# A hybrid attention and RG-LRU block on one core: the last recurrent block interleaved, silu products moved to the middle, y loaded into freed tiles, and two kinds of transfers given to other queues

## Chip, cores and metric

The kernel runs on one core of one Trainium2 chip. Its time is device microseconds (us) of one execution, median over several runs. The profile is one more execution, recorded by the hardware profiler.

The engines are named as in the profile: PE (TensorE matmuls), PEld (TensorE weight loads), DVE (VectorE), ACT (ScalarE), POOL (GpSimd), SP (SyncE, which here only issues DMA transfers; its instruction stream is SPq).

## What is computed

A sequence of 1024 tokens with 1024 channels goes through one decoder block and a final RMSNorm. Cut to what matters:

```python
h = rmsnorm(x, norm_g) * (1 + scale) + shift
q, k, v, g_attn, xr, g_rnn, m_attn, m_rnn = split(h @ w_in)      # 1024 x 6656
y_attn = sliding_window_attention_with_sinks(rope(q), rope(k), v) * silu(g_attn)
xr = causal_depthwise_conv(xr, conv_w, conv_b)                   # width 4
r = sigmoid(block_diag(xr, wa) + ba);  i = sigmoid(block_diag(xr, wx) + bx)
log_a = -8 * r * softplus(-lam);  a = exp(log_a)
b = sqrt(-expm1(2 * log_a)) * (i * xr)                           # reset at position 0
y_rnn = scan(h[t] = a[t] * h[t-1] + b[t]) * silu(g_rnn)
merged = sigmoid(m_attn) * (y_attn @ w_attn_proj) + sigmoid(m_rnn) * (y_rnn @ w_rnn_proj)
out = rmsnorm(x + gate * (merged @ w_out), final_g)
```

The attention window is 128 tokens in blocks of 128; there are 16 heads and 4 key/value heads. The recurrence has four blocks of 256 channels.

## The kernel before

Every large product is made of float32r parts: a tensor is split into a high part (a cast on ACT, names `wh`, `hh`, `yh`) and the rest (a subtraction on DVE, `wl`, `hl`, `yl`), and three matmuls, high by high, low by high and high by low, stand for one float32 product.

**The input projection** is cut into *pairs*: 23 pairs of 256 output columns, each computed by seven block products (a Strassen form on half sequences and half columns). One product is 12 matmuls at L505 and one *slot* of the planner. For each product DVE forms a sum `ws` (L527), ACT casts it to `wh` (L101) and DVE subtracts to `wl` (L107); the second matmul of the product needs `wl`. The list `pairs` (L1249) sets their order: Q (queries), MA and MR (merge gates, a tanh on ACT only), GR and GA (silu paths: a tanh on ACT and one more DVE operation at L613 for each of four tiles), XR (input of the recurrence).

**The recurrence** runs beside these products. After an XR pair, the convolution (L682 to L697) and the gate matmuls (L778, `pgate`, two sets of 24 per block: one for each half of the block's 256 channels) are followed for each half by `after_gates` (L785): sigmoids into `rz` and `it` (L793, L796), DVE products (L799, L803), tanh (L807), exp and square (L810, L813), DVE (L816), sqrt (L820), DVE (L823), the scan (L828), the product with the silu path `gg` (L832), and the split into `yh` (L835) and `yl` (L839), which are stored to `yh_d` and `yl_d`. Each step that changes ACT's function loads a table first. A planner (`background`, L468) places these steps between the products by its own estimates of load; the order on each engine is then fixed. In the last block (`hb == 3`) the second half's steps are listed behind all of the first half's.

**Attention** starts when the recurrence's steps are all issued (L1317 to L1320). Its tiles lie in the memory that the recurrence gives up. It has 32 steps u of one query block and one key/value head: scores (`s_ps`, L1016), masked maximum (L1024 to L1035), exponentials (L1040), transposition (`pt`, L1054), masks on GpSimd (`phm`, `plm`, L1074), and values (`pv`, L1088). In each step one *filler* product is put between: first the last products of the last pair, from the seventh step on the products of `w_rnn_proj` with `yh` and `yl` (L168, `rp`). For this, `load_y` (L1135) brings y back from DRAM: channel blocks 0 and 1 into halves of the `hha`/`hla` tiles, blocks 2 to 7 into twelve tiles of their own, which exist only once the input projection is done.

**Queues.** All transfers but a few are issued by SP in the program's order, and an SP instruction that waits holds up all behind it. In attention, stores of a product's tiles are put off to the end of a step (`store`, L590).

The tail is the product with `w_attn_proj` beside the merge (L1449 to L1481) and that with `w_out` (L1500), with the last norm.

Of the kernel before, what the change touches and what calls it, by code (L numbers as in the profile page):

```python
# [13 lines left out]
F32R = mybir.dt.float32r  # L14
# [8 lines left out]
P = 128  # L23
S = 1024
D = 1024
KC = 8
# [25 lines left out]
def tile_hybrid_block(ctx, tc, x, pk, rows, posr, posi, invf, c_row, w_ss, w_gate, w_main, w_v,  # L52
# [91 lines left out]
    hh, hl = [], []  # L144
    for kc in range(KC):
        for lst, nm in ((hh, "hh"), (hl, "hl")):
# [512 lines left out]
    def xr_sinks(hb):  # L659
# [15 lines left out]
        def conv(ic):  # L675
            def add(s):
# [25 lines left out]
                waiting[1].extend([[("A", 1.06, 0, base)], slots(1), *[[t_] for t_ in taps]])  # L702
# [44 lines left out]
    def start_gates(hb):  # L747
# [4 lines left out]
        one, two = [], [lambda: ask(hb, 1)]  # L752
        for todo, steps_ in ((one, c0), (two, c1)):
            for i, step in enumerate(steps_):
                todo.extend(step + ([slots(1)] if hb < 3 else []))
                if todo is one and i == 3:
                    todo.append(lambda: gq.append((hb, 1)) or True)
        if hb == 3:
            one.insert(0, lambda: W.setdefault("rush", True))
        waiting[0].extend(one + two)  # L760
# [24 lines left out]
    def after_gates(hb, oc):  # L785
        c, t = 2 * hb + oc, {}

        def tl(n, tag=None, dt=F32):
            t[n] = W["rn"].tile([P, S], dt, tag=tag or n, name=n)
            return t[n][:]  # L790

        def a1():
            A.activation(tl("rz"), W["g", (hb, oc)][0][:], AF.Sigmoid, bias=pcol(PK_BA, c))  # L793

        def a2():
            A.activation(tl("it"), W["g", (hb, oc)][1][:], AF.Sigmoid, bias=pcol(PK_BX, c))  # L796
# [5 lines left out]
        def d2():  # L802
            V.tensor_tensor(out=t["it"][:], in0=t["it"][:], in1=W["xc", hb, oc][2][:],  # L803
                            op=ALU.mult)

# [185 lines left out]
    def load_v(m):  # L991
# [143 lines left out]
    def load_y(c):  # L1135
# [7 lines left out]
        h_ = W["yp"].tile([P, S], F32R, tag="Y", name="yh")  # L1143
        l_ = W["yp"].tile([P, S], F32R, tag="Y", name="yl")
        dma(h_[:], yh_d[c])
        dma(l_[:], yl_d[c])
# [3 lines left out]
    def rp_steps():  # L1150
# [4 lines left out]
        W["yp"] = pool(ctx, "ypool", bufs=12)  # L1155
# [20 lines left out]
        load_y(2)  # L1176
# [72 lines left out]
    pairs = [Q[1], MA[0], Q[2], MA[1], Q[3],  # L1249
# [385 lines left out]
```

## Time and profile before

| | |
|---|---|
| median of 3 runs | 945.71 us (943.57 to 946.53) |
| the profiled execution: its time | 944.47 us |
| the profiled execution: its span | 942.5 us |
| PE busy | 908.1 us, 96% of the span |
| DVE, ACT, POOL busy | 73%, 56%, 10% |
| TensorE clock granted | 0.999 |
| DMA moved | 164.19 MB, mean 174 GB/s |

How to read the rows of a timeline: start in us from the span's start, duration in us, engine, line, operation, output<-input, shapes and count; in brackets how long the engine had been idle before it, and what ended that. A row of the windows view gives, for one stretch, its length and then, for PE, PEld, DVE, ACT and POOL, the busy us and the count of instructions; last come the granted clock, the share of time in which the 16 DMA engines were busy (it can pass 1 by rounding) and the GB/s. In a group row the count follows x, then busy us and the mean ns of one.

### The profile page before, as it was taken

To read this page: it belongs to the slowest core of one execution; us is meant where nothing else is said; L and a number is where in the kernel's file an instruction comes from. 1 tells how busy PE (TensorE), PEld (TensorE's weight loads), DVE (VectorE), ACT (ScalarE), POOL (GpSimd) and SP (SyncE) were. 2 spreads that over 40 slices of the span, in tenths; PEclk is the share of its full clock that TensorE was granted. 3 is DMA by queue.
4 is the path that set the end of the run, shared out by engine and by line. 5 is a ranking of instruction groups with operands and counts; after the bars stand their busy time and mean duration, and the time that the engine had idled before them with its cause. 6 is when DMAs were issued, how large, how long until landed. Compare 5 with 4: busy or idle time off the path is not lost.

```text
span 942.5 us, 12419 instructions
## 1 busy us (share of the span) xinstructions
PE 908.1 (96%) x4261; PEld 750.6 (80%) x4261; DVE 688.8 (73%) x1068; ACT 528.8 (56%) x1036; POOL 89.7 (10%) x129
## 2 busy tenths in 40 slices
PE   5899999999999999999999999989999999999997
PEld 3689777788888788888888778867888888887886
DVE  7977798876668955984688677888999737656522
ACT  7434654455556755866585775877888632212311
POOL 1056000000000000000000000233333300000000
PEclk9999999999999999999999999999999999999999
DMA  8923565753332433352334237897666286436321
GB/s 312 370 68 152 184 223 202 268 189 125 112 112 96 139 136 100 133 212 80 122 112 168 100 134 261 278 342 251 215 198 187 67 304 219 168 118 235 128 79 67
DMA packets 84275, 164.19 MB, mean 174 GB/s; under 512 B 12771, under 2 KB 33251, under 8 KB 84214
## 3 DMA queue, kind: packets, MB, share of 16 engines
q1 hardware_dynamic: 83350, 161.09, 49.8%
q0 software_dynamic: 720, 2.07, 0.6%
q8 instruction: 33, 0.54, 0.2%
q14 instruction: 28, 0.23, 0.1%
q10 hardware_dynamic: 144, 0.26, 0.1%
HBM read 114.00 MB, written 49.78 MB: 174 GB/s over the span
## 4 chain that ended last, share of the span: by engine, by line
PE 75%; ACT 4%; DMA 4%; DVE 4%; issue 2%; SPq 0%; POOL 0%; DVEq 0%; ACTq 0%
PE bk L505 39%; PE rp L168 12%; PE rp L1500 5%; PE pgate L778 5%; PE pmain L1500 4%; PE pmain L168 4%; PE s_ps L1016 3%; PE pv L1088 3%; PE pt L1054 1%; DMA dv<-dv_d 1%; DMA ks<-k_d 1%; DMA r<-w_rp 1%; ACT wh L101 1%; DMA r<-w_main 1%; DVE nl L390 1%
## 5 line engine op out<-in xcount | busy, mean ns | idle before, releaser
L505 PE MATMUL bk<-nh,wl 128*128 128x512 f32 x368 | 143.7, 391 | 2.0 <-DVE wl L107 1.9
L505 PE MATMUL bk<-nh,wh 128*128 128x512 f32 x368 | 143.4, 390 | 0.0
L505 PE MATMUL bk<-nl,wh 128*128 128x512 f32 x368 | 143.2, 389 | 0.0
L107 DVE TENSOR_TENSOR wl<-r,wh 128x512 fp32r<-128x512 f32 x108 | 79.1, 736 | 16.5 <-ACT wh L101 16.5
L101 ACT CAST wh<-r 128x512 fp32r<-128x512 f32 x108 | 66.5, 618 | 33.5 <-DMA r<-w_ap 11.3
L505 PEld LDWEIGHTS bk<-nh,wl 128*128 128x128 f32 x368 | 69.1, 188 | 17.7 <-DVE wl L107 3.1
L505 PEld LDWEIGHTS bk<-nh,wh 128*128 128x128 f32 x368 | 69.1, 188 | 15.2 <-ACT wh L103 0.9
L505 PEld LDWEIGHTS bk<-nl,wh 128*128 128x128 f32 x368 | 69.1, 188 | 14.3
L505 PE MATMUL bk<-hh,wl 128*128 128x512 f32 x184 | 71.7, 390 | 0.4 <-DVE wl L107 0.4
L505 PE MATMUL bk<-hl,wh 128*128 128x512 f32 x184 | 71.6, 389 | 0.0
L505 PE MATMUL bk<-hh,wh 128*128 128x512 f32 x184 | 71.6, 389 | 0.0
L107 DVE TENSOR_TENSOR wl<-ws,wh 128x512 fp32r<-128x512 f32 x80 | 54.1, 683 | 4.0 <-ACT wh L101 4.0
L101 ACT CAST wh<-ws 128x512 fp32r<-128x512 f32 x80 | 48.2, 616 | 4.8 <-DVE ws L527 3.0
L1040 ACT ACTIVATE p<-p,small 128x129 f32<-128x129 f32 x128 | 50.1, 400 | 0.0
L59 POOL DMA_DIRECT2D yh_d<-yh x1 | 0.6, 583 | 482.3 <-ACT yh L835 482.3
L505 PE MATMUL bk<-hha,wl 128*128 128x512 f32 x92 | 36.4, 395 | 5.9 <-DVE wl L107 4.4
L505 PEld LDWEIGHTS bk<-hh,wl 128*128 128x128 f32 x184 | 34.5, 188 | 7.9 <-DVE wl L107 0.8
L505 PEld LDWEIGHTS bk<-hh,wh 128*128 128x128 f32 x184 | 34.5, 188 | 7.2
L505 PEld LDWEIGHTS bk<-hl,wh 128*128 128x128 f32 x184 | 34.5, 188 | 7.1
L1016 PE MATMUL s_ps<-ks,qs 128*128 128x256 f32 (+1 forms) x256 | 37.5, 289 | 0.0
L1517 ACT ACTIVATE o<-xo 128x1024 f32<-128x1024 f32 (+2 forms) x10 | 8.9, 889 | 48.4 <-DVE xo L1516 48.4
L505 PE MATMUL bk<-hla,wh 128*128 128x512 f32 x92 | 35.9, 390 | 0.0
(338 smaller groups left out, 2231.7 us busy)
## 6 DMA issues: line engine op xcount, KB each, us to landing
r<-w_main SPq DMA_DIRECT2D x100, 256.0 KB, 4.0
wada<-w_ss SPq DMA_DIRECT2D x16, 512.0 KB, 8.6
qs<-q_d SPq DMA_DIRECT2D x16, 512.0 KB, 5.4
ks<-k_d SPq DMA_DIRECT2D x24, 192.0 KB, 4.1
xt<-x SPq DMA_DIRECT2D x8, 512.0 KB, 7.2
q_d<-rhi SPq DMA_DIRECT2D x16, 256.0 KB, 3.5
q_d<-rlo SPq DMA_DIRECT2D x16, 256.0 KB, 3.3
wg<-w_gate SPq DMA_DIRECT2D x8, 512.0 KB, 5.0
```

Source lines behind the costliest of these rows:

```text
L101: A.copy(dst[0][:], src)
L107: V.tensor_tensor(out=dst[1][:], in0=src, in1=f32(dst[0][:]), op=ALU.subtract)
L168: mm = T.matmul(ps[hf], ww, xx[kc][hf], start=(kc == 0 and ww is w_h and xx is xh), stop=(kc == KC - 1 and xx is xl))
L390: V.tensor_tensor(out=nl[t][:], in0=xT[t][:], in1=f32(nh[t][:]), op=ALU.subtract)
L505: W["pe"] = T.matmul(ps, ww[:, c], b[kc][xx_], start=(first and kc == 0 and i == 0), stop=(kc == 3 and i == 2), skip_group_check=not first)
L778: W["pe"] = T.matmul(ps[:, SL[hf]], ww[:, c0:c0 + P], xx_[:, SL[hf]], start=(ic == 0 and i == 0), stop=(ic == 1 and i == 2))
L1016: W["pe"] = T.matmul(o, qs[:, j, qc], ks[:, b, k0 + (0 if n else P):k0 + 256], start=(b == 0), stop=(b == 1))
L1040: A.activation(px[:, j, :], px[:, j, :], AF.Exp, bias=sm[:, 0, j:j + 1], accum_out=sm[:, 1, j:j + 1])
L1054: W["pe"] = T.transpose(pt[:, j, :], px[:, j, 0:P], ident[:])
L1088: W["pe"] = T.matmul(pv[:], b, m[:].rearrange("p j q -> p (j q)"), start=(i == 0), stop=(i == len(prods) - 1))
L1500: T.matmul(ps[:, sl], lhs[k][th][:, ts_], w[:, sl], start=(k == 0 and w is h_ and lhs is mh), stop=(k == KC - 1 and lhs is ml))
L1517: A.activation(o[:, sl], xo[:, sl], AF.Square, accum_out=fs[:, i:i + 1])
```

## The change

Six edits, on top of a kernel that computes the same.

1. **The order of the pairs.** The silu pairs GR and GA all stand before the last XR pair or directly ahead of it; MA[2], MA[3] and all MR follow it. One pair (now, as before, MR[3]) is left for attention.
2. **The last recurrent block.** The steps of its two halves are interleaved by a list written by hand, and the second half's `rz`, `it`, `th` and `av` take the buffers of the tags `xa` and `xcl` (convolution results, free after the gate matmuls) and no longer wait for the first half's.
3. **A guard**: a convolution waits in the planner until the buffer that it takes has been used (`W["used", c]`).
4. **y into h tiles.** The tiles `hh4` to `hh7` and `hl4` to `hl7` stay open to the end; y blocks 2 to 5 are loaded into them as soon as the input projection has read them, and block 2 is asked for in slot +6 of the last pair, before the `w_rnn_proj` products. In the tail the merged tensor's blocks 2 to 5 are written there too.
5. **v pieces** (`dv`, `vs`; 128 KB each) are loaded by GpSimd.
6. **Tanh stores in attention** (`smr_d`) are issued by ACT, directly behind the activation that makes the tile.

```diff
-    hb = h_ctx.enter_context(tc.tile_pool(name="hb", bufs=1))
+    hb = ctx.enter_context(tc.tile_pool(name="hb", bufs=1))
...
+                whole[nm, kc] = a[:]
...
-                        store(dst[j][:, SL[th]], t["t"])
+                        dma(dst[j][:, SL[th]], t["t"], A if "att" in W else nc.sync)
...
-                waiting[1].extend([[("A", 1.06, 0, base)], slots(1), *[[t_] for t_ in taps]])
+                waiting[1].extend([lambda: c < 2 or ("used", c - 2) in W,
+                                   [("A", 1.06, 0, base)], slots(1), *[[t_] for t_ in taps]])
...
+            waiting[0].extend(
+                [lambda: W.setdefault("rush", True), *a1, a2, d1,
+                 lambda: gq.append((hb, 1)) or True, a3, d2, a4, a5, lambda: ask(hb, 1), *b1,
+                 d3, b2, e1, b3, e2, b4, b5, a6, e3, d4, b6, d5, e4, d6, a7, e5, d7, e6, b7,
+                 e7])
...
+        beside = {"rz": "xa", "it": "xa", "th": "xcl", "av": "xcl"} if c == KC - 1 else {}
...
-        dma(dv[:], dv_d[g][:, n0:n0 + 2, :])
+        dma(dv[:], dv_d[g][:, n0:n0 + 2, :], G)
...
-        dma(vs[:, lo:, :], vs_d[g][:, n0 - 1 + lo:n0 + 1, :])
+        dma(vs[:, lo:, :], vs_d[g][:, n0 - 1 + lo:n0 + 1, :], G)
...
-        h_ = W["yp"].tile([P, S], F32R, tag="Y", name="yh")
-        l_ = W["yp"].tile([P, S], F32R, tag="Y", name="yl")
+        if c < 6:
+            h_, l_ = whole["hh", c + 2], whole["hl", c + 2]
+        else:
+            h_, l_ = (W["yp"].tile([P, S], F32R, tag="Y", name=n_)[:] for n_ in ("yh", "yl"))
...
-        W["yp"] = pool(ctx, "ypool", bufs=12)
+        W["yp"] = pool(ctx, "ypool", bufs=4)
...
-             XR[0], GR[0], GR[1], XR[1], MA[2], GR[2], MR[0], XR[2], MR[1], MR[2], MA[3],
-             XR[3], GR[3]] + GA + MR[3:]
+    pairs = [Q[1], MA[0], Q[2], MA[1], Q[3], XR[0], GR[0], GA[0], XR[1], GR[1], GA[1], GR[2],
+             XR[2], GA[2], GA[3], GR[3], XR[3], MA[2], MA[3]] + MR
...
-    at_slot(s_last + 2, ("N", 0, 0, lambda: load_r(0)), ("N", 0, 0, lambda: load_y(0)),
-            ("N", 0, 0, lambda: load_r(1)), ("N", 0, 0, lambda: load_y(1)),
-            ("N", 0, 0, lambda: prep_r(0, 0)), ("N", 0, 0, lambda: prep_r(1, 0)))
+    at_slot(s_last + 2, [("N", 0, 0, lambda: load_r(0)), ("N", 0, 0, lambda: load_y(0))],
+            ("N", 0, 0, lambda: load_y(1)), ("N", 0, 0, lambda: load_r(1)), [],
+            [("N", 0, 0, lambda: prep_r(0, 0)), ("N", 0, 0, lambda: load_y(2))],
+            ("N", 0, 0, lambda: prep_r(1, 0)))
...
-        if c < 2:
+        if c < 6:
             mh[c], ml[c] = yh[c], yl[c]
```

On PE the order from the first scores on is the same as before, product by product; between the last gate matmuls and the first scores stand 14 products where there were 12. In the instruction orders below, names carry buffer numbers where they are needed to tell tiles apart.

**First place: the DVE order in the second half's steps of the last recurrent block.** Before, from the second half's first product `rz` on (its operand comes from ACT):

```order
L799 SCALAR_TENSOR_TENSOR rz_4951<-rz_4951,pk_t_75,rbig_77 128x1024
L613 SCALAR_TENSOR_TENSOR c_4944<-c_4944,bk0_68 128x512
L565 TENSOR_TENSOR c_4970<-u2_4922,bk3_71 128x512
L107 TENSOR_TENSOR wl_4947<-r_4824,wh_4946 128x512
L527 TENSOR_TENSOR ws_4976<-ws_4949,r_4824 128x512
L803 TENSOR_TENSOR it_4953<-it_4953,xc_4427 128x1024
```

Now, from the second half's `th` on (`th_4914`, `rz_4888` and `it_4887` belong to the second half, `it_4759`, `th_4782` and `rz_4757` to the first):

```order
L836 SCALAR_TENSOR_TENSOR th_4914<-rz_4888,th_4914 128x1024
L843 SCALAR_TENSOR_TENSOR it_4759<-th_4782,it_4759 128x1024
L566 TENSOR_TENSOR c_4976<-u2_4933,bk3_71 128x512
L107 TENSOR_TENSOR wl_4955<-r_4835,wh_4954 128x512
L528 TENSOR_TENSOR ws_4982<-ws_4957,r_4835 128x512
L566 TENSOR_TENSOR c_5003<-bk1_69,p5_4883 128x512
L107 TENSOR_TENSOR wl_4979<-ws_4957,wh_4978 128x512
L528 TENSOR_TENSOR ws_5006<-r_4837,r_4835 128x512
L848 SCALAR_TENSOR_TENSOR rz_4757<-av_4788,it_4759 128x1024
```

The second half no longer begins behind the first half's last step; steps of both halves alternate, and `wl_4955`, of the sixth product after the last gate matmuls, stands behind two steps that wait for ACT.

**Second place: SP at the start of attention.** Each row is a transfer, with the semaphores for which SP waits ahead of it (DMAHW: transfers issued by SP or ACT, in a rotation of eight; DMASW: those issued by GpSimd, likewise; the others are engines). Before:

```order
L59 DMA sink<-rows 128x16 [waits DMASW5_49,DMAHW5_49,DMASW4_49,PE_49]
L59 DMA ks<-k_d 64x2x256 [waits DMASW7_49,DMAHW6_49,DMASW6_49,PE_49]
L59 DMA ks<-k_d 64x2x256 [waits DMAHW7_49]
L59 DMA qs<-q_d_93 128x4x256 [waits DMASW2_49,DMAHW0_49,DMASW1_49,DMASW0_49]
L59 DMA ks<-k_d 64x2x384 [waits DMAHW1_49]
```

Now:

```order
L59 DMA sink<-rows 128x16 [waits DMASW5_49,DMAHW7_49,DMASW4_49,DVE_49]
L59 DMA ks<-k_d 64x2x256 [waits DMASW7_49,DMASW6_49,DMAHW0_49,DMASW1_49,PE_49]
L59 DMA ks<-k_d 64x2x256 [waits DMAHW2_49]
L59 DMA qs<-q_d_93 128x4x256 [waits DMAHW3_49,DMASW2_49,DMASW0_49]
L59 DMA ks<-k_d 64x2x384 [waits DMAHW4_49]
```

GpSimd issues eight transfers early in the program, and the ninth and tenth are the stores of the last `yh` and `yl`, which raise DMASW0 and DMASW1 a second time. Before, every GpSimd transfer waited for here is one of the eight early ones, and PE is waited for at the last gate matmuls. Now the DVE instruction for which `sink` waits is the last block's `yl` subtraction, and the count of DMASW1 for which the first `ks` waits is the second one, the landing of the `yl` store: with edit 2 the memory that attention takes was last used by that tile.

**Third place: SP and the loads of y.** Before, the loads of y blocks 2 and 3 (`yh_d2`, `yl_d2`, `yh_d3`, `yl_d3`) stand behind the last stores:

```order
L59 DMA smr_d6_115<-c_5540 128x512
L59 DMA dv_5555<-dv_d0_88 128x256
L59 DMA vs_5554<-vs_d0_84 128x256
L59 DMA smr_d7_116<-c_5600 128x512
L59 DMA smr_d7_116<-c_5603 128x512
L59 DMA yh_5626<-yh_d2_119 128x1024
L59 DMA yl_5627<-yl_d2_127 128x1024
L59 DMA yh_5630<-yh_d3_120 128x1024
L59 DMA yl_5631<-yl_d3_128 128x1024
```

Now block 2 follows the key and query loads of steps 6 and 7 (`ks_5380`, `qs_5383`), and block 3 those of steps 8 and 9:

```order
L59 DMA r_5369<-ga_d0_97 128x2x256
L59 DMA ks_5380<-k_d_82 64x2x384 x2
L59 DMA qs_5383<-q_d0_93 128x4x256
L59 DMA hh4_174<-yh_d2_119 128x1024
L59 DMA hl4_175<-yl_d2_127 128x1024
L59 DMA r_5507<-ga_d0_97 128x2x256
L59 DMA ks_5518<-k_d_82 64x2x256 x2
L59 DMA qs_5521<-q_d1_94 128x4x256
L59 DMA hh5_176<-yh_d3_120 128x1024
L59 DMA hl5_177<-yl_d3_128 128x1024
```

Stores and v pieces no longer stand on SP, and the loads of y are earlier against the steps of attention.

More of the change, by code (lines that the diff above doesn't have):

```diff
@@ L140, in tile_hybrid_block @@
     h_ctx = ExitStack()
-    hb = h_ctx.enter_context(tc.tile_pool(name="hb", bufs=1))
+    hb = ctx.enter_context(tc.tile_pool(name="hb", bufs=1))
     b12_ctx = ExitStack()
     b12 = b12_ctx.enter_context(tc.tile_pool(name="b12", bufs=1, side="right"))
-    hh, hl = [], []
+    hh, hl, whole = [], [], {}
     for kc in range(KC):
@@ L804, in d2 @@
                             op=ALU.mult)
+            W["used", c] = True
         def a3():
@@ L1142, in load_y @@
             return
-        h_ = W["yp"].tile([P, S], F32R, tag="Y", name="yh")
-        l_ = W["yp"].tile([P, S], F32R, tag="Y", name="yl")
-        dma(h_[:], yh_d[c])
-        dma(l_[:], yl_d[c])
+        if c < 6:
+            h_, l_ = whole["hh", c + 2], whole["hl", c + 2]
+        else:
+            h_, l_ = (W["yp"].tile([P, S], F32R, tag="Y", name=n_)[:] for n_ in ("yh", "yl"))
+        dma(h_, yh_d[c])
+        dma(l_, yl_d[c])
         yh[c] = [h_[:, SL[0]], h_[:, SL[1]]]
```

33 lines of the change are left out of this document (20 added, 13 removed).

## The prediction

> **What bounds the kernel.** First the page's head, its slices, and the windows view for the stretches that the change touches.
>
> ```profile
> span 942.5 us, 12419 instructions
> PE 908.1 (96%) x4261; PEld 750.6 (80%) x4261; DVE 688.8 (73%) x1068; ACT 528.8 (56%) x1036; POOL 89.7 (10%) x129
> DMA  8923565753332433352334237897666286436321
> ...
> 350.00:400.00 50.00, 50.00 (x222) 41.37 (x221) 37.00 (x48) 35.27 (x48) 0.00 (x0) 1.00 0.33 110
> 524.00:577.00 53.00, 49.70 (x215) 39.45 (x214) 41.65 (x53) 38.07 (x52) 1.31 (x3) 1.00 0.46 162
> 580.00:584.00 4.00, 4.00 (x23) 3.44 (x22) 3.21 (x5) 1.81 (x7) 0.44 (x3) 1.00 0.40 152
> 584.00:604.00 20.00, 20.00 (x114) 17.21 (x112) 18.03 (x35) 16.68 (x57) 3.60 (x7) 1.00 1.00 313
> 604.00:612.00 8.00, 8.00 (x47) 6.97 (x46) 6.51 (x13) 7.27 (x21) 2.69 (x5) 1.00 0.54 180
> 612.00:640.00 28.00, 23.57 (x124) 18.31 (x122) 23.10 (x41) 18.35 (x63) 7.92 (x13) 1.00 1.03 349
> ```
>
> PE is busy 96% of the span, and without a gap in a quiet stretch such as 350 to 400. The change takes no matmul away, so it can only win what PE waits: 942.5 - 908.1 = 34.4 us, most of it at the start and end, which no edit touches. Two places matter: 524 to 577, the last recurrent block (3.3 us idle), and 612 to 640, early attention (4.4 us idle), where the DMA engines are full, while they stood half empty from 604 to 612 and at 0.40 around 582.
>
> A wait costs a little more than its idle time, as the pipelined matmuls start anew. The timeline of PE at the first wait, and then all others from 300 to 577:
>
> ```profile
> 529.51 0.39 PE L505 MATMUL bk<-nh,wh 128*128 128x512 f32 x1
> 530.53 0.50 PE L505 MATMUL bk<-nh,wl 128*128 128x512 f32 x1 [0.63 <-DVE wl L107]
> 530.87 0.40 PE L505 MATMUL bk<-nl,wh 128*128 128x512 f32 x1
> ...
> 550.94 0.50 PE L505 MATMUL bk<-hha,wl 128*128 128x512 f32 x1 [1.08 <-DVE wl L107]
> 560.87 0.50 PE L505 MATMUL bk<-nh,wl 128*128 128x512 f32 x1 [1.23 <-DVE wl L107]
> 567.01 0.50 PE L505 MATMUL bk<-hh,wl 128*128 128x512 f32 x1 [0.35 <-DVE wl L107]
> ...
> 325.58 0.50 PE L505 MATMUL bk<-hha,wl 128*128 128x512 f32 x1 [0.45 <-DVE wl L107]
> ```
>
> Matmuls that do not wait start about 50.00 / 222 = 0.23 us apart. From 529.51 over 530.53 to 530.87 pass 1.36 us in place of 0.45: 0.91 us lost for 0.63 idle, 0.28 more. The last block thus loses 0.63 + 1.08 + 1.23 + 0.35 + 4 x 0.28 = 4.4 us. Each time `wl` was late, and DVE was late because it stood in front of a step that waits for ACT.
>
> **The last block now** (edits 1 and 2). I walk through both engines by the new order. Their spacings, from the second half's steps before the change:
>
> ```profile
> 547.67 1.11 ACT L796 ACTIVATE it<-pgate,pk_t 128x1024 f32<-128x1024 f32 x1
> 559.36 1.28 ACT L820 ACT_TABLE_LOAD   x1
> 560.66 1.06 ACT L820 ACTIVATE th<-th 128x1024 f32<-128x1024 f32 x1
> 561.75 1.23 DVE L823 SCALAR_TENSOR_TENSOR it<-th,it 128x1024 f32<-128x1024 f32 x1 [0.33 <-ACT th L820]
> 562.89 0.68 DVE L107 TENSOR_TENSOR wl<-r,wh 128x512 fp32r<-128x512 f32 x1
> 563.49 2.29 DVE L828 TENSOR_TENSOR_SCAN rz<-av,it 128x1024 f32<-128x1024 f32 x1
> ```
>
> So from start to start: an ACT step of 1024 columns about 1.05, a table load 1.3, a cast 0.5; on DVE 1.14, 0.6 for 512 columns, 2.2 for a scan. Let T be the end of the last gate matmuls. ACT: `rz` and `it` to 2.1; the tanh sink of the product that runs first after T cannot start before 3.0 (a product is 12 x 0.227 = 2.72); cast, `th`, cast; the copy of the second product's result at 5.7; table, exp, square to 9.7; sink, cast, and the next table from 10.65; the first half's sqrt from 11.95 to 13.0. DVE has been waiting in front of `it_4759` since 10.9; that step takes 13.0 to 14.15, a join to 14.8, and `wl_4955` is there at 15.5. Its product, the sixth after T, wants it at 5 x 2.72 + 0.23 = 13.8. **One wait of 1.7 us** remains, 2.0 with the restart. Ahead of T the long steps lie at least one product ahead of their `wl`, and after 15.5 each `wl` comes 0.5 to 1.8 us before its product. Term: 4.4 - 2.0 = **2.4 us won**; bounds 4.4 (no wait) and -1 (as many waits again, which the old order shows to be possible).
>
> From 14.8 to the end stand twelve steps of 0.6, four of 1.14 and two scans: 16.2 us; then `yh` on ACT (1.1) and `yl` on DVE (1.2), which ends at T + 32.2. PE is ready for the first scores after 14 products and the wait: T + 40.0, **7.8 us** later.
>
> **The start of attention** (new wait, from edit 2's buffers). As the second order shows, the first `ks` now waits until the `yl` store has landed. Before, it did not:
>
> ```profile
> 567.38 1.26 SPq L59 DMA_DIRECT2D ks<-k_d  x2
> 569.27 1.22 DVE L839 TENSOR_TENSOR yl<-rz,yh 128x1024 fp32r<-128x1024 f32 x1
> 570.80 0.54 POOL L59 DMA_DIRECT2D yl_d<-yl  x1 [0.68 <-DVE yl L839]
> 577.84 1.00 PE L1016 MATMUL s_ps<-ks,qs 128*128 128x128 f32 x8
> ...
> yl_d<-yl SPq DMA_DIRECT2D x7, 512.0 KB, 2.6
> yl_d<-yl POOLq DMA_DIRECT2D x1, 512.0 KB, 7.2
> ...
> DMA to landing us min/median/max: 4.0/5.4/8.9
> ```
>
> The loads left at 567.38, before `yl` was even computed; the trace thus has 7.35 us from the end of `yl` (570.49) to the scores, of which none was needed. Now the chain is: 0.3 to GpSimd's issue, the store's landing, 0.1, 1.26 for two `ks` issues, the landing of `qs` (the last row is that of `qs`). The store takes 2.6 (same size, issued by SP) to 7.2 (the one that GpSimd issued, while the loads that SP had sent from 567.38 on were under way). I take 3.5, near the first, because SP now has nothing to send meanwhile; for `qs` 4.7, between least and median. Sum 0.3 + 3.5 + 0.1 + 1.26 + 4.7 = 9.9, against 7.8: PE waits **2.1 us**. Bounds: 0.3 + 2.6 + 0.1 + 1.26 + 4.0 - 7.8 = 0.5, and with 7.2 and 8.9, 10.0. Behind the waiting SP stand `w_rp`, y and all later loads; they shift with it.
>
> The Trainium skill, DMA: Bandwidth & Descriptors, section on the anatomy of one DMA on the SWDGE (gpsimd) path, gives 2.0 us plus bytes / 436e3 per transfer, by estimate 3.2 us for 512 KB; the trace's 7.2 disagrees, under load. By the page the wait would be 1.8 us.
>
> **Early attention** (edits 4, 5, 6).
>
> ```profile
> 608.89 1.56 SPq L59 DMA_DIRECT2D smr_d<-c  x2
> 610.50 0.42 SPq L59 DMA_DIRECT2D yh<-yh_d  x1
> ...
> 614.32 1.09 PE L1016 MATMUL s_ps<-ks,qs 128*128 128x128 f32 x8
> 617.85 0.73 PE L168 MATMUL rp<-yh,wh 128*128 128x512 f32 x2 [0.48 <-DMA yh<-yh_d]
> 626.90 0.47 PE L1088 MATMUL pv<-phc,vs 128*128 128x512 f32 x1 [1.44 <-DVE small L1035]
> 639.05 0.47 PE L1088 MATMUL pv<-phc,dv 128*128 128x512 f32 x1 [1.82 <-DMA dv<-dv_d]
> 639.95 1.19 PE L1016 MATMUL s_ps<-ks,qs 128*128 128x256 f32 x8
> 644.99 1.19 PE L1016 MATMUL s_ps<-ks,qs 128*128 128x256 f32 x8
> ...
> 604.25 0.39 POOL L1004 COPY p<-sink 128x4 f32<-128x4 f32 x1 [2.02 <-PE pt L1054]
> ```
>
> A quiet step takes 644.99 - 639.95 = 5.04 us; the four from 614.32 to 639.95 took 25.63, so **5.4 us** were lost. SP stood at the store until 608.89; then y blocks 2 to 7, 6 MB, left from 610.50 on into full DMA engines. The windows show the room missed: (349 - 180) x 8 + (349 - 152) x 4 = 2.1 MB, 6.0 us at 349 GB/s. Now no store blocks SP, and blocks 2 and 3 (2 MB) leave when PE has read `hh4` in the fourth step (some 16 us after the first scores) and behind the next keys (some 24 us), in place of 32.7 us. That takes 2 MB out of the full stretch, enough for all 5.4. Against it, the first keys and queries (1.7 MB) now leave about 5 us nearer to the scores, part of which the gap at 580 swallows. I take 1.4 lost, **4.0 won**; bounds 0 and 5.4. v: GpSimd has 2.02 us free between mask and sink copy, two issues take 0.58 + 0.54; nothing. ACT's stores wait for the transfer eight back, a load issued many us earlier; behind them wait a cast and the next step's copy of `s_ps`; nothing, at most 2 us where y or r lands late.
>
> **The middle.** In 300 to 500 four silu pairs more give DVE 16 steps of 0.6 among its 0.74 load (37.00 of 50). The old first block, with two silu pairs beside it, had one wait of 0.45 (+0.28); three such blocks now: 0.5 lost, bounds -0.7 (none) and 3 (waits as in the last block). The tail's orders are unchanged: 0. Edit 3 costs nothing: it moves steps, no engine waits for it.
>
> **Sum**: 2.4 - 2.1 + 4.0 - 0.5 = 3.8 us won: 944.47 - 3.8 = 940.7 for the profiled execution. That one lies 1.24 below the median of its runs, so 941.9, rounded to **942.0**.
>
> **Rivals.**
> 1. *The DMA engines are the bound, not SP.* All bytes of y, keys and v are still needed by the same step, and 612 to 640 stood at 1.03; then term three is 0: 944.7, on the median's scale 945.9. For it: the later start of the keys. Against it: 2.1 MB of unused room. The skill's DMA: Bandwidth & Descriptors, section "Issuing engines are not separate DMA queues", speaks for it: several issuers share 16 engines and save only issue time; the shares of 1.00 and 1.03 agree.
> 2. *The wait at the first scores decides* and makes it **slower**: store 7.2, `qs` 8.9, wait 10.0 in place of 2.1: 948.6, or 949.8. From a wait of 2.1 + 3.8 + 2.8 = 8.7 us on it is slower by more than 0.3%. For it: the only GpSimd store of this size took that long. Against: it met a full DMA queue.
> 3. *The waits move to the middle*: 3 us in place of 0.5: 943.2, or 944.4.
>
> **How the numbers follow.** Forecast 0.52, with a range of its own of 939 to 944.5; rivals 0.22, 0.14, 0.12. A measurement here tells about 0.3%, 2.8 us, from no change, so faster means below 942.9: most of the forecast, a little of rival 3: 0.47. Rival 1, the rest of both: same 0.38. Rival 2: slower 0.15. The range runs from 938.5 (no wait in the last block, all 5.4 won, little of the rest) to 948.5, which leaves out most of rival 2 and a little below.
>
> **What would show it.** After the last gate matmuls one wait for `wl` of about 1.7 us, in the sixth product; SP's first `ks` after the `yl` store has landed, and PE idle some 2 us before the first `s_ps`; y blocks 2 and 3 issued some 16 and 24 us after it; about 21.5 us for the four steps that took 25.63; `dv` and `vs` never awaited. Wrong would be: a first-scores wait over 5 us, waits for `yh` or `ks` from the ninth step on, or several `wl` waits between 300 and 520.

## The result, and the profile after

The changed kernel takes 952.97 us (median of 5 runs, 950.14 to 953.43), the kernel before 944.04 (943.57 to 946.53): a ratio of 1.0079 with a 95% interval of 1.0057 to 1.0100. It is **slower**, by 0.8%; the forecast was 942.0, a little faster. The profiled execution took 953.21. Lines that stood at L505 in the kernel before stand at L506 here.

The page's head and, from the windows view, four stretches of the changed kernel:

```profile
span 951.5 us, 12417 instructions
PE 913.6 (96%) x4261; PEld 754.7 (79%) x4261; DVE 688.5 (72%) x1068; ACT 529.5 (56%) x1036; POOL 109.8 (12%) x161
```

```profile
350.00:400.00 50.00, 48.09 (x203) 38.87 (x203) 30.34 (x38) 30.08 (x41) 0.00 (x0) 0.97 0.24 85
450.00:500.00 50.00, 48.09 (x203) 38.86 (x202) 33.56 (x41) 33.94 (x45) 0.00 (x0) 0.97 0.29 98
550.00:600.00 50.00, 44.37 (x193) 36.49 (x192) 30.02 (x39) 27.09 (x47) 3.71 (x8) 0.93 0.61 206
600.00:650.00 50.00, 49.45 (x274) 41.87 (x273) 45.05 (x83) 41.75 (x135) 22.17 (x36) 1.00 0.98 330
```

Two things stand out. PE starts only 203 matmuls in 350 to 400, where the kernel before had 222 and no gap; and PE's *busy* time has grown by 5.5 us (908.1 to 913.6) though the matmuls are the same. The clock column tells why: 0.97, 0.97, 0.93 in three stretches that read 1.00 before. Matmuls ran slower there. In 600 to 650, on the other hand, PE is now busy 49.45 of 50 us.

The ledger, on the span (951.5 against 942.5, 9.0 us), from the PE timelines of both kernels: middle, 8.1 lost (two places of 4.07, worked out below, and 0.65 at 514 us, less 0.73 before); last block, 2.5 won; wait at the first scores 4.2 lost (4.05 of it idle), and 3.15 more behind it; early attention 4.9 won; start and tail 0.9 lost together.

**The middle.** PE's timeline; in brackets the idle time and what ended it:

```profile
376.75 0.39 PE L506 MATMUL bk<-hla,wh 128*128 128x512 f32 x1
377.59 0.49 PE L506 MATMUL bk<-nh,wh 128*128 128x512 f32 x1 [0.45 <-ACT wh L101]
379.54 0.73 PE L506 MATMUL bk<-nh,wl 128*128 128x512 f32 x1 [1.46 <-DVE wl L107]
380.07 0.63 PE L506 MATMUL bk<-nl,wh 128*128 128x512 f32 x1
380.50 0.63 PE L506 MATMUL bk<-nh,wh 128*128 128x512 f32 x1
...
383.06 0.40 PE L506 MATMUL bk<-nh,wh 128*128 128x512 f32 x1
```

The product waits for its `wh` and again for its `wl`, 0.45 + 1.46 = 1.91 us in all, and then its matmuls start 0.43 us apart in place of 0.23, until 383. From 376.75 to the third matmul of the next product pass 7.47 us (to 384.22), where 15 steps of 0.227 make 3.40: **4.07 us lost**, of which the late operands are 2.4 and the slow matmuls 1.6. The same happens at 468.90 and 470.85, with the same numbers. Why `wh` was late stands on ACT; the last line is the same copy in the kernel before:

```profile
360.67 0.59 ACT L555 COPY u<-bk 128x512 f32<-128x512 f32 x1
372.46 0.59 ACT L671 COPY xr<-bk 128x512 f32<-128x512 f32 x1 [11.20 <-PE pgate L791]
372.94 0.62 ACT L101 CAST wh<-r 128x512 fp32r<-128x512 f32 x1
373.58 1.28 ACT L830 ACT_TABLE_LOAD   x1
374.88 1.06 ACT L830 ACTIVATE av<-rz 128x1024 f32<-128x1024 f32 x1
375.97 1.06 ACT L833 ACTIVATE rz<-av 128x1024 f32<-128x1024 f32 x1
376.93 0.60 ACT L101 CAST wh<-ws 128x512 fp32r<-128x512 f32 x1
...
369.21 0.59 ACT L670 COPY xr<-bk 128x512 f32<-128x512 f32 x1 [5.19 <-PE bk L505]
```

ACT stands 11.2 us in front of the copy of XR[2]'s first result. The copy goes into a buffer of tag `xa`, which still holds a converted input of block 1, and the gate matmuls (`pgate`) have to read that first. When ACT is free, a table load, an exponential and a square stand ahead of the cast that PE needs. Before, the gates had read that buffer, ACT waited 5.2 us for the product itself, and no wait on PE followed.

**The start of attention**, timelines of DVE, POOL, SP and PE, in order of time:

```profile
574.84 1.22 DVE L859 TENSOR_TENSOR yl<-rz,yh 128x1024 fp32r<-128x1024 f32 x1
576.37 0.54 POOL L59 DMA_DIRECT2D yl_d<-yl  x1 [0.68 <-DVE yl L859]
582.20 1.27 SPq L59 DMA_DIRECT2D ks<-k_d  x2
583.58 0.54 SPq L59 DMA_DIRECT2D qs<-q_d  x1
588.06 1.94 PE L1036 MATMUL s_ps<-ks,qs 128*128 128x128 f32 x8 [4.05 <-DMA qs<-q_d]
```

The chain is the one forecast: 0.31 to GpSimd's issue, 5.83 to the first keys, 1.38 for two issues, 4.48 until `qs` is there, 12.0 us in all. PE was ready 7.95 us after `yl`, at 584.01.

### The profile page after: what moved, and what is told of

Its sections match the earlier page's. It is cut to its first block, busy times and chain, and to the rows that moved or that the text cites. A ratio compares the mean times of both kernels' runs of the same rounds, so it can differ in the third digit from the quotient of the medians.

```text
span 951.5 us, 12417 instructions
## 1 busy us (share of the span) xinstructions
PE 913.6 (96%) x4261; PEld 754.7 (79%) x4261; DVE 688.5 (72%) x1068; ACT 529.5 (56%) x1036; POOL 109.8 (12%) x161
## 4 chain that ended last, share of the span: by engine, by line
PE 66%; DVE 11%; DMA 7%; ACT 4%; issue 3%; SPq 0%; POOL 0%; ACTq 0%; DVEq 0%
PE bk L506 39%; PE rp L169 9%; PE pgate L791 4%; PE rp L1521 3%; PE pmain L1521 3%; PE s_ps L1036 3%; DMA wo<-w_out 3%; PE pv L1108 2%; DMA tt<-tr_d 1%; DVE wl L107 1%; PE pt L1074 1%; PE pmain L169 1%; DMA smr<-smr_d 1%; DVE wo L1457 1%; DVE wo L1453 1%
## 5 line engine op out<-in xcount | busy, mean ns | idle before, releaser
L506 PE MATMUL bk<-nh,wl 128*128 128x512 f32 x368 | 146.1, 397 | 3.4 <-DVE wl L107 3.3
L506 PE MATMUL bk<-nh,wh 128*128 128x512 f32 x368 | 145.7, 396 | 0.9 <-ACT wh L101 0.9
L506 PE MATMUL bk<-nl,wh 128*128 128x512 f32 x368 | 145.4, 395 | 0.0
L506 PEld LDWEIGHTS bk<-nh,wl 128*128 128x128 f32 x368 | 70.4, 191 | 19.8 <-DVE wl L107 4.6
L506 PEld LDWEIGHTS bk<-nh,wh 128*128 128x128 f32 x368 | 70.5, 192 | 17.4 <-ACT wh L101 1.8
L506 PEld LDWEIGHTS bk<-nl,wh 128*128 128x128 f32 x368 | 70.4, 191 | 14.5
L506 PE MATMUL bk<-hh,wh 128*128 128x512 f32 x184 | 71.6, 389 | 0.0
L506 PE MATMUL bk<-hh,wl 128*128 128x512 f32 x184 | 71.6, 389 | 0.0
L506 PE MATMUL bk<-hl,wh 128*128 128x512 f32 x184 | 71.6, 389 | 0.0
L506 PE MATMUL bk<-hha,wl 128*128 128x512 f32 x92 | 36.5, 397 | 6.3 <-DVE wl L107 4.8
L506 PEld LDWEIGHTS bk<-hh,wh 128*128 128x128 f32 x184 | 34.5, 188 | 7.1
L506 PEld LDWEIGHTS bk<-hl,wh 128*128 128x128 f32 x184 | 34.5, 188 | 7.1
L506 PEld LDWEIGHTS bk<-hh,wl 128*128 128x128 f32 x184 | 34.6, 188 | 7.1
L1036 PEld LDWEIGHTS s_ps<-ks,qs 128*128 128x128 f32 x256 | 33.3, 194 | 5.0 <-issue 4.4
L506 PE MATMUL bk<-hha,wh 128*128 128x512 f32 x92 | 35.8, 390 | 0.0
```

What stands on the lines that cost most here:

```text
L506: W["pe"] = T.matmul(ps, ww[:, c], b[kc][xx_], start=(first and kc == 0 and i == 0), stop=(kc == 3 and i == 2), skip_group_check=not first)
L1036: W["pe"] = T.matmul(o, qs[:, j, qc], ks[:, b, k0 + (0 if n else P):k0 + 256], start=(b == 0), stop=(b == 1))
```

## The experiments

All ratios are to the kernel before on the same chip. Where two intervals overlap, the runs do not tell the two kernels apart.

| run | what | median us | ratio (95%) |
|---|---|---|---|
| e1 | before + edits 4, 5, 6 | 940.51 | 0.9958 (0.9939 to 0.9978) |
| e2 | changed, edit 2 undone | 949.09 | 1.0052 (1.0032 to 1.0072) |
| e3 | changed, last y in other buffers | 950.12 | 1.0051 (1.0022 to 1.0080) |
| e4 | changed, two MA pairs moved back | 950.37 | 1.0060 (1.0039 to 1.0081) |
| e5 | e1, gates held back | 956.44 | 1.0129 (1.0111 to 1.0146) |
| e6 | changed, gates earlier | 947.34 | 1.0034 (1.0019 to 1.0048) |
| e7 | before + pauses, one run | 962.91 | |
| e8 | before + edit 6 | 941.37 | 0.9975 (0.9961 to 0.9989) |
| e9 | changed, first scores later | 951.96 | 1.0085 (1.0068 to 1.0101) |
| e10 | e6 and e9 together | 951.28 | 1.0080 (1.0065 to 1.0096) |
| e11 | before + edit 4 | 940.00 | 0.9957 (0.9940 to 0.9973) |
| e12 | changed, SP stores the last y | 952.09 | 1.0090 (1.0073 to 1.0108) |
| e13 | before + edits 4, 5 | 941.59 | 0.9963 (0.9950 to 0.9977) |
| e14 | e10, edit 6 undone | 945.83 | 1.0012 (0.9999 to 1.0025) |

### Which edits won and which lost: e1 and e2

e1 takes the changed kernel and undoes edits 1, 2 and 3; e2 undoes edit 2 alone (`beside` and the interleaved list).

> The kernel before with edits 4, 5 and 6 alone (y into freed h tiles, v by GpSimd, stores by ACT); old pair order, old last block, no guard. Theory (each edit acts by itself; what was lost lies in edits 1 and 2): early attention gives back the 4.9 us that the profile of the changed kernel shows from its second scores to its last, so 944.5 - 4.9 = 939.6, between 938.5 and 941; the four waits of the last block (3.3 us idle) stay, there is no wait at the first scores. Rival (the gain of early attention came from the loads that the late start had already finished): 943 to 945, with waits for yh or dv after the eighth step.

> The changed kernel with edit 2 undone: the last block's halves one behind the other, in buffers of their own; new pair order, guard, 4, 5 and 6 stay. Theory (the buffers of edit 2 make the first keys wait for a store): the wait of 4.05 us at the first scores and the low clock behind it (3.15 us) both go, some 2 us come back as waits in the last block: 953.2 - 7.2 + 2.5 = 948.5; the two pairs of waits near 378 and 469 us stay, each with its stretch of low clock. Rival (the first scores wait because early attention's loads were put elsewhere): the wait stays and the time is 953 or more.

Both came out as the theory had it. From e1 to e2 only edits 1 and 3 are added, and the guard moves no instruction under the old order: **the new pair order costs 8.6 us** (940.51 to 949.09). Edit 2 costs the rest, some 2.5 us by the ratios and 4 by the medians, net of what it wins; the intervals of e2 and the changed kernel overlap, so this part is not clear of noise. In e2 PE does not wait at the first scores; the two pairs of waits in the middle stand as in the changed kernel. But e2 changes the cover too: there `yl` ends at 574.52, 12.2 us ahead of the scores at 586.68, and a chain of 12.0 us, as in the changed kernel, would just have fitted. So e2 alone does not show that the wait came from the buffers; the first keys' departure 0.07 us after the landing of the `yl` store (582.13), and e3 below, do.

### The middle: collision or load? e4, e5, e6

Two causes fitted the trace. The XR copy collides with gates that come later now; or the silu pairs simply load DVE too much. e4 moves pairs, so it changes both; e5 and e6 change one without the other.

```diff
# e4
-XR[1], GR[1], GA[1], GR[2], XR[2], GA[2], GA[3], GR[3], XR[3], MA[2], MA[3]] + MR
+XR[1], GR[1], MA[2], GA[1], XR[2], GR[2], MA[3], GA[2], XR[3], GR[3], GA[3]] + MR
# e5, in conv (on e1, with the guard)
-waiting[1].extend(split0 + [lambda: start_gates(hb)])
+waiting[1].extend(split0 + ([slots(5)] if hb == 1 else [slots(4)] if hb == 2 else [])
+                  + [lambda: start_gates(hb)])
# e6, in start_gates; in conv also the slots(1) around base, hi and lo left out for hb 1, 2
-                    if todo is one and i == 3:
+                    if todo is one and i == (2 if hb in (1, 2) else 3):
```

> The changed kernel with another pair order: MA[2] and MA[3] go back between the recurrent blocks, GA[2] moves one place, GR[3] and GA[3] go behind XR[3] (XR[1], GR[1], MA[2], GA[1], XR[2], GR[2], MA[3], GA[2], XR[3], GR[3], GA[3], MR). Six silu pairs in place of eight stand before the last XR pair, and by the planner the second gate matmuls of blocks 1 and 2 come ahead of the next XR pair's first result copy again. Theory (ACT stands in front of that copy until the gates have read its buffer): the waits near 378 and 469 us and the low clock behind them go, 2 x 4.07 us: 945.1; up to 2 us more in the last block, which has two silu pairs beside it. So 945 to 947; the wait at the first scores stays. Rival (the silu pairs simply load DVE too much): several shorter waits between 300 and 520, 949 or more.

> The kernel of e1 (edits 4, 5, 6, old pair order, old last block) with one thing added: the planner holds the gates of block 1 back by five slots and those of block 2 by four (and the guard of edit 3, without which the steps would block each other). The silu pairs stay where they were before; the second gate matmuls of blocks 1 and 2 now come one product after the next XR pair's first result copy, as in the changed kernel. Theory (ACT stands in front of that copy until the gates have read its buffer, and then three long steps come ahead of the next product's cast): two pairs of waits as in the changed kernel, each 1.9 us idle and 2.4 with the restarts, 4.1 where the low clock follows: 940.5 + 5 to 8 = 945.5 to 948.5. Rival (the eight silu pairs in the middle load DVE too much): no silu pair is moved, so 940.5, within 1 us.

> The changed kernel, pair order and all else as they are, but in blocks 1 and 2 the planner's pauses of one slot between the convolution's steps are left out and the second gate set is asked for one step earlier, so that both sets stand ahead of the next XR pair's first result copy. Theory (collision of gates and copy): the waits near 378 and 469 us go, with the low clock behind them: 953.0 less 5 to 8 = 945 to 948; the wait at the first scores stays. Rival (silu pairs load DVE): the waits stay or move, 951 or more.

e5, with no silu pair moved; PE's timeline at the first place, then ACT's ahead of it:

```profile
378.58 0.49 PE L506 MATMUL bk<-nh,wh 128*128 128x512 f32 x1 [0.44 <-ACT wh L101]
380.53 0.50 PE L506 MATMUL bk<-nh,wl 128*128 128x512 f32 x1 [1.46 <-DVE wl L107]
...
373.45 0.59 ACT L671 COPY xr<-bk 128x512 f32<-128x512 f32 x1 [9.91 <-PE pgate L780]
```

The same two waits, within 0.01 us, under the old order. And e6, the new order with the gates ahead of the copy; windows, then ACT's timeline at the copy:

```profile
350.00:400.00 50.00, 49.49 (x218) 40.43 (x217) 33.95 (x44) 31.96 (x44) 0.00 (x0) 1.00 0.24 87
450.00:500.00 50.00, 50.00 (x220) 40.90 (x219) 36.91 (x45) 38.04 (x50) 0.00 (x0) 1.00 0.29 100
```

```profile
366.61 0.59 ACT L671 COPY xr<-bk 128x512 f32<-128x512 f32 x1 [2.29 <-PE pgate L792]
```

218 and 220 matmuls in place of 203, and ACT stands 2.3 us in place of 11.2. **The collision is the cause**: made in one kernel and taken away in the other, with DVE's busy time the same in all four (e1 688.4 us, e5 688.7, changed 688.5, e6 688.5). What is left beside it is small: e6 keeps three waits (0.51, 1.16 and 0.26). The profiled execution of e6 is the fastest of its ten (944.10, with a clock of 0.998); the others had 0.993 to 0.997, so they saw more of the low clock than these windows show. The pair order made the collision because the planner, with more DVE work booked between, let the convolution's steps and so the gates come three products later (block 1's second set stands behind 90 of these products, before behind 87), while the XR pairs kept their places. e5 as a whole missed its range (956.44 against 945.5 to 948.5): its last block, whose second gates come a product later, waits 1.02, 0.19, 0.82, 0.71 and 2.85 us, and the first scores 0.67.

e4 missed its theory (950.37 against 945 to 947). The two pairs of waits are gone there too, and three short ones stand between 400 and 505 (0.40, 0.41 and 0.57). But PE reached the first scores earlier and the chain did not, so the win was given back there:

```profile
586.62 0.66 PE L1036 MATMUL s_ps<-ks,qs 128*128 128x128 f32 x2 [6.82 <-DMA qs<-q_d]
```

### The start of attention: e3, e12, e9, e10, e14

e3 puts the last `yh` and `yl` where the first half's `rz` and `th` were; e12 lets SP issue their two stores (the diff shows one); e9 begins attention three products later (the loop is put behind the `at_slot` calls).

```diff
# e3
-"av": "xcl"} if c == KC - 1 else {}
+"av": "xcl", "rz7": "rz", "th7": "th"} if c == KC - 1 else {}
-A.copy(tl("yh", "av", F32R), t["rz"][:])
+A.copy(tl("yh", "av" if c < KC - 1 else "rz7", F32R), t["rz"][:])
-V.tensor_tensor(out=tl("yl", "it", F32R), in0=t["rz"][:], in1=f32(t["yh"][:]),
+V.tensor_tensor(out=tl("yl", "it" if c < KC - 1 else "th7", F32R), in0=t["rz"][:], in1=f32(t["yh"][:]),
# e12
-dma(yl_d[c], t["yl"][:], G if c == KC - 1 else nc.sync)
+dma(yl_d[c], t["yl"][:], nc.sync)
# e9
-    while W["slot"] < 7 * (len(pairs) - N_ATT) + 1:
+    while W["slot"] < 7 * (len(pairs) - N_ATT) + 4:
```

> The changed kernel, but the last yh and yl lie in buffers of the first half (rz and th), so that the memory of the first keys was last read by a DVE step and not by a store. Same instructions in the same order on every engine. Theory (landing of the yl store is the wait): the first keys leave about 6 us earlier, right behind the yl subtraction, qs lands before PE wants it (or up to 0.5 us late), no low clock: 953.2 - 7.2 = 946.0, between 945 and 947.5. Rival (the transfers of keys and queries are slow by themselves, or SP is held up by something else): PE still waits 2 us or more and the time is above 949.

> The changed kernel, but SP and not GpSimd issues the stores of the last yh and yl; the first keys still wait for them. Theory (GpSimd's store takes 5.8 us to land, where SP's stores of this size take 2.6 in the middle of the changed kernel): the first keys leave about 2.5 to 3 us earlier, the wait at the first scores falls from 4.05 to between 1 and 2.5 (qs may take longer, as in e3), the low clock may or may not follow: 948 to 951. Rival (the landing time comes from the size and the traffic, not from the queue): the wait stays at 3.5 to 4.5 and the time at 952 to 953.5.

e3's timelines of DVE, SP and PE:

```profile
575.99 1.23 DVE L860 TENSOR_TENSOR yl<-rz,yh 128x1024 fp32r<-128x1024 f32 x1
577.74 1.56 SPq L59 DMA_DIRECT2D ks<-k_d  x2
579.47 1.42 SPq L59 DMA_DIRECT2D qs<-q_d  x1
587.25 0.97 PE L1037 MATMUL s_ps<-ks,qs 128*128 128x128 f32 x7 [2.16 <-DMA qs<-q_d]
```

In both the keys left earlier, as the theory had it, and the time did not follow: 950.12 and 952.09, with waits of 2.16 and 3.77 at the first scores, are the rivals' numbers. In e3 the keys no longer wait for the store, and leave 0.5 us behind `yl`; but now `qs` takes 7.8 us to arrive in place of 4.5, while the two stores of 0.5 MB are under way (the last lands at 583.52). In e12 the `yl` store landed in 3.6 us, the keys left 3.7 us after its issue in place of 5.8, and `qs` took 6.6. There both stores had landed by 578.76, before `qs` left at 580.28, and `dv` and `vs` left beside it at 580.42 and 581.00; so the stores are not the whole reason why `qs` is slower, and what is was not separated. The chain from the end of `yl` to the scores was 12.0, 10.0 and 11.7 us in the changed kernel, e3 and e12: what one transfer won the next gave back in part. In e1 the keys depend on `yl` no more than in the kernel before (they leave at 567.06, `yl` ends at 570.18), and PE does not wait.

> The changed kernel with attention's first scores put three products later (products that would have been fillers in the last steps of attention); all else as it is, the keys still wait for the yl store. Theory (the chain from the end of yl over the store, the first keys and qs takes about 12 us and only lacks cover): three products are 8.2 us, more than the wait of 4.05, so PE does not wait there, no low clock follows, and 7.2 us come back: 953.0 - 7.2 = 945.8, between 945 and 947.5. Rival (the chain's lateness is passed on to the loads behind it, r and y): the wait at the first scores goes, but waits for r, yh or yl appear in the steps after it, 948 or more.

> Both repairs on the changed kernel: gates of blocks 1 and 2 earlier (e6) and the first scores three products later (e9). If the two losses are separate, e6's 947.3 less the wait of 3.15 at the first scores and some 1.9 of low clock behind it: 942.2, between 940 and 943.5; faster than the kernel before by 1 to 4 us, about as fast as e1 (940.5), since the last block gains 2.5 us but two waits of 0.5 and 1.2 are new in the middle. Rival (they are not separate, a part returns elsewhere): 945 or more.

Both missed, and came out as their rivals had it. The wait at the first scores was gone, but e10's ACT and PE timelines show a new one behind it:

```profile
580.61 0.60 ACT L609 ACTIVATE c<-bk 128x512 f32<-128x512 f32 x1 [2.13 <-PE bk L506]
588.63 0.33 ACTq L59 DMA_DIRECT2D smr_d<-c  x1
589.00 0.62 ACT L101 CAST wh<-ws 128x512 fp32r<-128x512 f32 x1 [7.79 <-DMA hha<-yh_d]
...
589.67 0.80 PE L506 MATMUL bk<-hh,wh 128*128 128x512 f32 x1 [2.81 <-ACT wh L101]
```

The tile was finished at 581.2, but ACT could issue its store only at 588.63: a store issued by ACT waits for a transfer issued eight before it, here one of SP's late loads, which landed at 588.56. ACT stands at such a store again until 611.21, and PE waits 1.74 us at 613.31; e9 has the same two places, with waits of 1.12 and 1.41. Near the end of attention, where the three products now lack as fillers, PE waits 1.43 us twice. e14 undoes edit 6 in e10:

> The kernel of e10 (gates earlier, first scores three products later) with edit 6 undone: SP issues the tanh stores again, at the end of a step. In e10 ACT stood 7.8 us at such a store, PE waited 2.8 us for the cast behind it. Theory (the store on ACT passes the lateness of SP's loads on to ACT): that wait goes with the low clock behind it, some 4 to 5 us; the two waits of 1.43 us near the end of attention, where fillers are lacking, stay: 951.3 - 4.5 = 946.8, between 945 and 948.5. Rival (the late loads hold up something else instead, SP's stores or the casts of r): 950 or more.

945.83: neither the wait of 2.81 nor one at the first scores is left, and the two of 1.43 stay; two short ones for y are new (0.53 and 0.77). So the store on ACT had taken back 5.5 us by the medians, 6.4 by the ratios. With both losses mended the kernel is level with the one before (1.0012, interval 0.9999 to 1.0025), while edits 4 and 5 alone took 941.59 on the same chip (e13): the new order and the new last block still cost 4.2 us.

### Early attention: e8, e11, e13

> The kernel before with edit 6 alone: ACT issues the tanh stores in attention. Theory of the prediction (SP stood at a store until 609 us and the y loads left only then): SP no longer stands there, but y still has to wait for tiles that exist only when the input projection is done, so part of the 4.9 us at most: 1 to 2 us faster, 942 to 943. Rival (the held up store was the whole delay): 940.5 as with all three edits. Other rival (only the tiles count): 943.5, no change.

> The kernel before with edit 4 alone: y blocks 2 to 5 into h tiles, block 2 asked for in the last pair. Theory (after e8: the store that holds SP up is the whole delay of early attention): SP still stands at that store until about 609 us, so the y loads leave no earlier and the waits for yh, yl, vs and dv stay: 943.5 to 945, no change within 1 us. Rival (the loads ahead of the block 2 load are put ahead of the store, which spreads the bytes): 940.5 to 942.

> The kernel before with edits 4 and 5, without edit 6. Theory (a store issued by ACT waits for a transfer issued long before it, 2.4 us at 595 us in e1 and e8, and takes back part of what edits 4 and 5 give): without it ACT never stands there, the steps five to nine of attention run as in e11, and the time is that of e11 or up to 1 us less (v leaves GpSimd while SP stands at its store): 939 to 940.5. Rival (edit 6 is needed with the others): 942 or more, with waits for yh, vs or dv.

e8's median lies between its theory and its first rival, but its profile is that of the rival: from the first scores to the last it takes 154.1 us, as e1 does, where the kernel before took 157.0. e11 went with its rival (940.00, where that had 940.5 to 942), e13 missed (waits of 0.34 and 1.47 for `yh` and `yl` at 637 and 640 us were left). Edit 6 alone, edit 4 alone, 4 with 5, and all three give 0.9957 to 0.9975, one result within the intervals. **Each of the edits 4 and 6 by itself ends most of the jam**, edit 6 by taking the store off SP (the y loads of block 2 leave at 603.95 and not 610.50), edit 4 by taking block 2 ahead of it (595.10); the gains do not add. Edit 5 alone was not run. In e1 this stretch is 2.9 us shorter than before, not the 4.9 of the changed kernel: from the second scores to the last it takes 150.4 us in e1, 148.7 in e2 and 148.4 in the changed kernel, where attention starts later. So some 2 of the 4.9 came only in the kernels with the later start, as e1's rival had it for all of it; what brought them was not separated. Nor is edit 6 free; ACT in e8:

```profile
592.76 0.59 ACT L608 ACTIVATE c<-bk 128x512 f32<-128x512 f32 x1
595.36 0.34 ACTq L59 DMA_DIRECT2D smr_d<-c  x1
595.80 0.37 ACT L1097 COPY ob<-pv 64x256 f32<-64x256 f32 x1 [2.45 <-DMA r<-ga_d]
```

In e8 that step of attention took 6.1 us (593.53 to 599.61) in place of 5.04. Edit 4 alone (e11, 0.9957) and edit 6 alone (e8, 0.9975), a single line, are the simplest kernels that beat the kernel before.

### The low clock: e7

```diff
+more = {(1, "S3"): 3, (3, "S3"): 5, (5, "S3"): 4, (6, "S3"): 6, (7, "S3"): 3, (8, "S3"): 5,
+        (9, "S3"): 4, (10, "S3"): 7, (11, "S3"): 3, (12, "S3"): 6, (13, "S3"): 4,
+        (14, "S3"): 5, (15, "S3"): 8}.get((s // 7, n), 0)
-return "D", 0, 0.69, lambda: rest(O[n], R[n], sc)
+return "D", 0, 0.69, lambda: [rest(O[n], R[n], sc) for _ in range(1 + more)]
```

> The kernel before, with the subtraction that makes the seventh product's wl done three to eight more times over (same values) in 13 of the pairs, so that PE pauses for different lengths, about 0.5 to 4 us, in stretches that had no wait. Theory on the low clock (it follows when PE was idle for more than about half of a fixed raster of some 3.4 us, as 92.3 us = 27 x 3.42 between its two beginnings in the changed kernel suggest): pauses under 1.7 us never bring it, pauses over 3.4 us always, those between only by where they fall; it ends some 3.4 or 6.8 us later. Rival (it follows on the length of the pause alone, with a sharp threshold between 1.6 and 1.9 us): pauses sort by length.

DVE had more slack than I thought, so few pauses came: 0.44 us twice, 1.26 twice, and 5.60 and 4.19. Windows of e7 around the first of 1.26 and that of 5.60:

```profile
305.00:308.00 3.00, 1.74 (x8) 1.10 (x7) 2.93 (x6) 0.75 (x2) 0.00 (x0) 1.00 0.01 3
330.00:333.00 3.00, 1.36 (x3) 1.16 (x4) 2.93 (x5) 0.62 (x1) 0.00 (x0) 0.56 0.00 0
333.00:336.00 3.00, 3.00 (x8) 2.31 (x7) 2.73 (x5) 2.10 (x3) 0.00 (x0) 0.50 0.43 171
```

Behind 1.26 the clock stayed at 1.00, behind 5.60 it was halved, as both theories have it. What tells them apart are the other runs, in the last section.

## Why the prediction was wrong

- **The middle** is the step that failed: "three such blocks now: 0.5 lost, bounds -0.7 and 3"; it lost **8.1 us**, with several `wl` waits between 300 and 520, which the prediction had named as the sign. I priced the silu pairs as load on DVE, from the one wait of the old first block, and gave no term to what the moved steps hold up. In the order of the new program, which I had, the second gate set of block 1 already stood behind XR[2]'s first product, and the copy of that product goes into a buffer which those gates read. I had looked at the engines' loads there, and not at which instruction holds a buffer that a moved one needs. Beyond that, a wait was priced at its idle time plus 0.28; the low clock behind it cost 1.6 more each time, which the trace of before never showed.
- **The start of attention**: mechanism right, size wrong. 2.1 was forecast, within bounds of 0.5 and 10.0; 4.2 came as wait (the store took 5.8, where I took 3.5 by SP's stores, though the GpSimd row said 7.2), and 3.15 more as low clock, for which the sum had no term: the first step took 6.82 us (588.06 to the next scores at 594.88) and not 3.67. The cover of 7.8 us came out (7.95), but by luck: 14.8 + 16.2 + 1.1 + 1.2 is 33.3 and not the 32.2 of the prediction, which left out the 1.1 of `yh`, and the steps were shorter by as much (`yl` ended 32.0 after the gates). The Trainium skill, DMA: Bandwidth & Descriptors, section on the anatomy of one DMA on the SWDGE (gpsimd) path, had given an estimate of 3.2 us for this store; the trace disagrees, with 5.8 here and 4.1 for `yh`. Rival 2 had the right place; it gave 10.0 for both and alone would have made 948.6.
- **The last block** was right: one wait, 2.5 won against 2.4.

```profile
559.45 0.50 PE L506 MATMUL bk<-hha,wl 128*128 128x512 f32 x1 [1.58 <-DVE wl L107]
```

  It is in the sixth product after the last gates, with 1.86 us in all where 2.0 were forecast.
- **Early attention** was right in size (4.9 against 4.0; block 2 of y left 17.8 and block 3 27.4 us after the first scores, against some 16 and 24), and rival 1 fell: at a DMA share of 0.98 in 600 to 650 PE hardly waits. The rule of the Trainium skill that spoke for it (DMA: Bandwidth & Descriptors, "Issuing engines are not separate DMA queues"), several issuers on the same 16 engines, agrees with that share; it did not make the wait. The size was partly luck: the three edits alone gave 2.9 in e1's profile, and some 2 came only with the later start. The reason was too narrow as well: the three edits were taken to share the gain, and each of 4 and 6 alone brings most of it.
- **Edit 6's wait**, "nothing, at most 2 us", was 0 in the changed kernel, 2.45 us of ACT in e8 (where the step grew by 1.0) and 7.8 in e10 (5.5 to 6.4 us of time), so the bound was too low.
- With the middle at 8.1 and the first scores at 7.35, the sum is 2.5 - 7.35 + 4.9 - 8.1 = -8.05; the start (0.36, nearly all from a wait at 120 us that was 0.3 longer) and the tail (0.57) make up the 9.0.

## What to carry to other kernels

When a list of work is reordered, look on each engine for an instruction that writes a buffer which a moved step has still to read: one blocked copy at the head of a queue cost far more here than the load that the move added (8.1 us in two places, where 0.5 was set down for the load). In this kernel a wait on PE costs its idle time and a little more, and where the idle time within one step of 3.4 us passes about half, 1.6 us of halved clock as well; so two short waits close together are worth more care than two far apart. Three edits that relieve the same jam are one gain, and a transfer given to a compute engine makes that engine stand wherever the transfer has to wait (ACT 7.8 us in e10).

## What the hardware did that was not expected

The granted clock goes to 0.50 behind a wait of PE as short as 1.8 us (1.81 in e3, at 120.62). In the profiles that have such stretches ahead of their last microseconds (the changed kernel, e2 to e7, e9, e10, e12 and e14) their ends lie on a raster wherever one run has more than one: in the changed kernel they are 92.2 and 119.5 us apart, 27 and 35 times 3.41, and in the others within 0.2 us of a multiple of it. The low stretches in the middle last one step of it, that behind the first scores of the changed kernel two. Counted in these steps, from 20 us on and up to the last product ahead of attention, every low stretch that began there followed a step with 1.73 us idle or more, and steps with up to 1.70 had none; one with 1.89 in the changed kernel had none either, and stays an exception. At the first scores and in attention, where many short matmuls run, four followed steps with 1.59 to 1.70 (e3, e9, e10 and e14). So the limit is not sharp in these rows, and length alone does not decide: a single wait of 1.85 us brought it in e4 and one of 2.31 at the same place in e5 did not; and the very same pair, 0.45 and 1.46, brought it at 380 us in the changed kernel but not at 381 in e3:

```profile
379.59 0.49 PE L506 MATMUL bk<-nh,wh 128*128 128x512 f32 x1 [0.46 <-ACT wh L101]
381.54 0.50 PE L506 MATMUL bk<-nh,wl 128*128 128x512 f32 x1 [1.46 <-DVE wl L107]
381.88 0.40 PE L506 MATMUL bk<-nl,wh 128*128 128x512 f32 x1
382.11 0.39 PE L506 MATMUL bk<-nh,wh 128*128 128x512 f32 x1
```

The Trainium skill, TensorE: Matmul & The Clock Gate, Part 1, states a free-running window of 3413 ns and two clocks, half and full; these traces agree (3.41 us; 0.50 and 1.00). Its section "Why this matters for your kernels" asks for no idle gap over about 3 us; here 1.9 us, in two pieces, were enough. That the share of about half of a step decides is worked out from these rows; no run here varied it by itself. It also gives a reason why runs of one kernel lie up to 6 us apart. In e3 the run of 944.67 had a granted clock of 0.999, and the four from 948.17 to 950.92 had 0.992 to 0.994, so the spread goes with the clock; that it is the place of the raster which differs from run to run was not tested.
